# Hybrid encoder layer: u and Toeplitz loads by four groups, first state copies directly behind the scan, last key's scaling put behind the first weight splits

## Chip, core and metric

The kernel runs on one NeuronCore of a Trainium2 chip, as one program with one launch. The core has a matmul engine (TensorE, PE), a vector engine (VectorE, DVE), a scalar engine (ScalarE, ACT), a general engine (GpSimd, POOL) and a sync engine (SyncE, SP). They run side by side, each through its own list of instructions in order, and wait for each other on semaphores. Transfers are issued by SP, ACT and POOL and carried by 16 DMA engines that all three share. The metric is device time in microseconds of one execution. All data are 32-bit floats; products are made exact enough by splitting each operand into a high and a low part and adding three matmuls.

## What is computed

An encoder layer on two sequences of 512 tokens of width 1024: an S5 state-space branch beside windowed attention, then an MLP. What the change touches is the state-space branch and the norm of the keys:

```python
proj = h @ w_in
q, k, v, u, g_att, g_ssm = jnp.split(proj, IN_SPLITS, axis=-1)
k = rms_norm(k.reshape(bsz, seq_len, N_KV_HEADS, HEAD_DIM), k_gain)
...
bu_re = jnp.einsum('lgc,gpc->lgp', us, bb_re[d])
bu_im = jnp.einsum('lgc,gpc->lgp', us, bb_im[d])
_, _, h_re, h_im = lax.associative_scan(_complex_combine, (ar, ai, bu_re, bu_im),
                                        reverse=reverse, axis=0)
return (jnp.einsum('lgp,gcp->lgc', h_re, cr[d])
        - jnp.einsum('lgp,gcp->lgc', h_im, ci[d]))
...
y = jax.nn.gelu(lax.map(one_seq, u))
```

There are 64 groups of 16 channels with 64 states each, in two directions.

## The kernel before

The state-space branch is computed in chunks of 8 tokens. Within a chunk the outputs come from a Toeplitz matrix of each group (`toep`, written to DRAM earlier as `toep_scr`) times the inputs `u_sb`; what comes from earlier chunks is a table `ctab` times the chunk states `h`. The states come from a scan over 64 chunks on VectorE (L619 to L624, four instructions a step, 62 steps). Then the readout loop (L644 on) takes two groups at a time, 32 readouts `q`: `state_rows(q)` copies the states of two groups out of `h` into a tile `st` (L632 and L636 on VectorE, L634 on ScalarE for even `q`; for odd `q` VectorE copies both halves); TensorE multiplies `toep` with `u_sb` (L655) and `ctab` with `st` (L658) into a PSUM tile `sps`, of which there are two; ScalarE applies the Gelu (L665) into `ys`, and stores it (L640) after every second readout. State tiles are made two readouts ahead.

The loads of the loop are issued by POOL. `load_batch` (L598) loads `u_sb` and `toep` of eight groups, 512 KB each, into two buffers each; `load_table` (L607) loads `ctab` of four groups, 512 KB, into three buffers. Two batches and three tables are loaded ahead of the scan; then each load is issued when a batch (four readouts) or a table (two readouts) has been used. Each of them waits for TensorE to have read the buffer that it fills.

Between those matmuls TensorE works off a generator of filler products, `fillers()` (L248): columns of the input projection (L185; three products of column parts, with 24 matmuls each for one sequence), then the keys (L225). `pull(n)` takes n units of it, two for a column matmul and one for a key matmul. In a column, `split` (L167) casts a raw weight block to its high part on ScalarE (`c_hi`, L175) and subtracts it on VectorE (`c_lo`, L176). A product ends with a copy on ScalarE out of one of three PSUM tiles `acc` (L200 or L202). Behind the scan 64 units are pulled, then `state_rows(0)` and `state_rows(1)` are issued, then the loop begins. Two weight splits lie in those 64 units.

The keys come in eight tiles of 128 tokens. For each, ScalarE squares (L234), VectorE sums (L236), POOL adds and takes the power -1/2 (L238, L239), and VectorE scales (L242). The scaling of one tile is issued in the middle of the next tile's matmuls; that of the last one directly at its end. Then the first query and value weights are loaded and split (`whole_block`, L985; `w_hi` on ScalarE, `w_lo` L993 on VectorE), and the keys are copied by DMA to `kn` (L999).

In the readout loop the order of each engine but SP and POOL is the order of the code; at the keys' end and the first weights a scheduler sets the order, and on SP and POOL it does so throughout the loop.

Of the kernel before, what the change touches and what calls it, by code (L numbers as in the profile page):

```python
# [12 lines left out]
F32 = mybir.dt.float32  # L13
# [6 lines left out]
P = 128  # L20
# [5 lines left out]
NSEQ = 2  # L26
# [12 lines left out]
GROUPS = 64  # L39
STATE = 64  # L40
CH = 16
T = 8
NCHUNK = SEQ // T
SB = 8
SI = 4
SG = 4
SH = 2
# [16 lines left out]
def hybrid_layer(ctx, tc, x, rel, onehot, w_qkv, w_ug, vectors, lam, coefs, w_glu, w_out, ln2,  # L64
# [82 lines left out]
    dmask = vec_pad[:, 72:72 + CH]  # L147
    lbt = cf.tile([P, 2, SB, 64], F32, name="lbt")
    columns = [("u", U_BLK + c) for c in range(KT)] + [("a", GA_BLK + c) for c in range(KT)] + [("s", GS_BLK + c) for c in range(KT)]
    loaded, key_tiles, sigmoids = [], [], set()  # L150
    phase = {"next": 0, "raw": [], "units": 2 * 3 * KT * NSEQ * len(columns) + 3 * KT * NT, "gelu": False}

    def fetch():
# [60 lines left out]
    def key_products():  # L214
        later = None
        for t in range(NT):
            if t % 4 == 0:
                key_tiles.append(evp.tile([P, 4, N_KV, HD], F32, tag="ev", name="keys"))
            kt = key_tiles[-1][:, t % 4]
            ps = acc()[:, 0:CB]  # L220
            for n in range(3 * KT):
                k, p = divmod(n, 3)
                hi, lo = loaded[len(columns) + k // 4]
                act, wt = [(0, hi), (0, lo), (1, hi)][p]
                PE.matmul(ps, hT[t // 4][act][:, k, (t % 4) * P:(t % 4 + 1) * P], wt[:, k % 4, :],  # L225
                          start=n == 0, stop=n == 3 * KT - 1)
                if t == 0 and n in (2, 6):
                    split(n // 6)
                if n == 12 and later:
                    later()  # L230
                if n < 3 * KT - 1:
                    yield 1
            psv = ps.rearrange("p (h d) -> p h d", h=N_KV)
            S.activation(kt, psv, AF.Square, scale=HD ** -0.5)  # L234
            ms = small.tile([P, N_KV], F32, tag="ms", name="ms")
            V.reduce_sum(ms, kt, axis=AX.X)  # L236
            rk = small.tile([P, N_KV], F32, tag="rq", name="rk")
            GP.tensor_scalar_add(ms, ms, EPS)  # L238
            GP.tensor_tensor(rk, ms, neg_half[:, 0:N_KV], op=ALU.pow)  # L239

            def later(kt=kt, psv=psv, rk=rk):
                V.tensor_mul(kt, psv, rk[:, :, None].to_broadcast([P, N_KV, HD]))  # L242

            if t == NT - 1:
                later()
            yield 1

    def fillers():  # L248
# [18 lines left out]
    def pull(units):  # L267
        while units > 0:
            cost = next(filler, None)
            if cost is None:  # L270
                return
            units -= cost
            phase["units"] -= cost
# [175 lines left out]
    with tc.tile_pool(name="hst", bufs=1) as hp:  # L449
# [147 lines left out]
        with tc.tile_pool(name="ssmo", bufs=2) as sp:  # L597
            def load_batch(g0):  # L598

                u_sb = sp.tile([P, SB, NSEQ * NCHUNK], F32, tag="u_sb", name="u_sb")  # L600
                GP.dma_start(u_sb, u_scr[g0:g0 + SB].rearrange("g c t k -> (c t) g k"))
                toep = sp.tile([P, SB, T, CH], F32, tag="toep", name="toep")
                GP.dma_start(toep.rearrange("p g t c -> p g (t c)"),
                             toep_scr[:, :, g0:g0 + SB].rearrange("c t g n -> (c t) g n"))
                return u_sb, toep

            def load_table(g0):  # L607
                ctab = sp.tile([P, SI, 2, T * CH], F32, tag="ctab", name="ctab_in", bufs=3)
                GP.dma_start(ctab.rearrange("p g r n -> p (g r n)"),
                             ct_scr[:, g0:g0 + SI].rearrange("p g r n -> p (g r n)"))  # L610
                return ctab

            ahead = [load_batch(0)]
            ahead_c = [load_table(0), load_table(SI), load_table(2 * SI)]
            ahead.append(load_batch(SB))
            GP.dma_start(line_scr, line_one[:, None, :].to_broadcast([N_HEADS, P, LINE]))
            order.close()
            order.enter_context(tc.manual_schedule(engines={mybir.EngineType.PE, mybir.EngineType.Activation, mybir.EngineType.DVE}))
            for i in range(1, NCHUNK - 1):  # L619
                t1, t2 = [sp.tile([P, 2, GROUPS, NSEQ], F32, tag="st", name=n, bufs=3) for n in ("t1", "t2")]  # L620
                V.tensor_mul(t1, h[:, i], a8r)  # L621
                V.tensor_mul(t2, h[:, i, ::-1], a8i)
                V.tensor_add(t1, t1, h[:, i + 1])
                V.tensor_add(h[:, i + 1], t1, t2)  # L624
                pull(15)
            phase["gelu"] = True
            pull(64)
            def state_rows(q):
                st = sp.tile([P, 2, SH, NSEQ, NCHUNK], F32, tag="st", name="st", bufs=3)
                hv = h[:, :, :, q * SH:(q + 1) * SH, :].rearrange("p k r g s -> p r (g s) k")  # L630
                sv = st.rearrange("p r g s k -> p r (g s) k")
                V.tensor_copy(sv[64:128], hv[64:128, :, :, ::-1])  # L632
                if q % 2 == 0:
                    S.copy(sv[0:64], hv[0:64])  # L634
                else:
                    V.tensor_copy(sv[0:64], hv[0:64])  # L636
                return st

            def store_y(y, ga):
                S.dma_start(y_scr[:, :, ga:ga + SI].rearrange("t c g k -> (t c) (g k)"), y.rearrange("p g k -> p (g k)"))  # L640

            states = [state_rows(0), state_rows(1)]
            full = None
            for q in range(GROUPS // SH):  # L644
                g0 = q * SH
                if g0 % SB == 0:
                    u_sb, toep = ahead.pop(0)
                if g0 % SI == 0:
                    ctab = ahead_c.pop(0)
                    ys = sp.tile([P, SI, NSEQ * NCHUNK], F32, tag="ys", name="ys", bufs=3)  # L650
                st = states.pop(0)
                ps = sps()
                for g in range(SH):
                    o = ps[:, g * P:(g + 1) * P]
                    PE.matmul(o, toep[:, g0 % SB + g].rearrange("p t c -> p (t c)"), u_sb[:, g0 % SB + g, :],  # L655
                              start=True, stop=False)
                    for ri in range(2):
                        PE.matmul(o, ctab[:, g0 % SI + g, ri, 0:T * CH],  # L658
                                  st[:, ri, g].rearrange("p s k -> p (s k)"), start=False, stop=ri == 1)
                if q + 2 < GROUPS // SH:  # L660
                    states.append(state_rows(q + 2))
                if full:
                    store_y(*full)
                    full = None
                S.activation(ys[:, g0 % SI:g0 % SI + SH].rearrange("p g k -> p (g k)"), ps[:, 0:SH * P], AF.Gelu_apprx_tanh)  # L665
                if (g0 + SH) % SI == 0:
                    full = ys, g0 + SH - SI

                pull(-(-(phase["units"] - 84) // (GROUPS // SH - q)))
                if (g0 + SH) % SI == 0 and g0 + SH + 2 * SI < GROUPS:  # L670
                    ahead_c.append(load_table(g0 + SH + 2 * SI))
                if (g0 + SH) % SB == 0 and g0 + SH + SB < GROUPS:
                    ahead.append(load_batch(g0 + SH + SB))
            store_y(*full)
            pull(phase["units"])
            order.close()
# [67 lines left out]
    with tc.tile_pool(name="att", bufs=2, reuse_waits="tile") as ap, tc.tile_pool(name="attc", bufs=1, reuse_waits="tile") as ac:  # L744
# [240 lines left out]
        def whole_block(src, pool, tag, bufs):  # L985
            halves = []
            for e in range(2):
                hi, lo = [pool.tile([P, KT // 2, CB], F32R, tag=t, name=n) for t, n in (("c_hi", "w_hi"), ("c_lo", "w_lo"))]
                raw = ap.tile([P, KT // 2, CB], F32, tag=tag, name="w_in", bufs=bufs)
                SP.dma_start(raw, src[:, e * 4:e * 4 + 4, :])  # L990
                for sl in (slice(0, 2), slice(2, 4)):
                    S.copy(hi[:, sl, :], raw[:, sl, :])
                    V.tensor_sub(lo[:, sl, :], raw[:, sl, :], hi[:, sl, :].bitcast(F32))  # L993
                halves.append((hi, lo))
            return halves


        for sq in range(NSEQ):
            SP.dma_start(kn[:, sq * 4:sq * 4 + 4], key_tiles[sq])  # L999
        kd = key_copies(0, 0)  # L1000
        w_q = whole_block(w_qkv[Q_BLK], wq, "ya", 2)
        weights[0] = w_q
        w_v = whole_block(w_qkv[V_BLK], cpool, "p", 3)
        load_biases(0)
        rows = None
        for t in range(4):
# [653 lines left out]
```

## Time and profile before

| what | value |
|---|---|
| median of three runs | 1470.34 us (1469.9 to 1470.96) |
| the profiled execution | 1471.94 us |
| its span | 1470.2 us, 22081 instructions |
| scan on VectorE (first and last start of L621) | 214.1 to 324.4 us |
| readouts on TensorE (first and last start of L655) | 325.9 to 405.3 us |
| u_sb, toep and ctab_in loads by POOL | 8, 8 and 16, 512 KB each |
| median time of these to landing | 7.3, 8.1 and 6.9 us |

The span runs from the first to the last instruction; the execution's own time has a little around it. Times in the rows that the prediction shows are microseconds from the span's start. A row of the order of time is: start, busy time, engine, line, operation, output <- inputs, shapes, and in brackets the idle time before it with what ended it. A row of waits is: who waited <- for whom: total us, times, longest. A row of windows is: window, its length, busy us (and instructions) of PE, PEld, DVE, ACT and POOL, then the clock that TensorE was granted, the mean busy share of the DMA engines, and GB/s. A row of DMA issues is: output <- input, queue, kind, count, size of one, us from issue to landing.

### The profile page before, as it was taken

Reading aid. Unit: us, or ns where it says so; the run is one execution under the profiler, and the core shown is the slowest. Engines: PE = TensorE matmul, PEld = TensorE weight load, DVE = VectorE, ACT = ScalarE, POOL = GpSimd, SP = SyncE. Lnnn points to the kernel's source line nnn. Section 1 sums busy time; section 2 is a strip of 40 time slices with the busy share of each in tenths; the row PEclk is TensorE's granted clock in tenths of the full one; section 3 lists DMA queues with packets and bytes.
Section 4 is the critical chain, followed back from the end, with each engine's and each line's share of the span. In section 5 each row is a group of like instructions: output and inputs, shape, how many; then the busy total and the mean of one; then the engine's idle time right before and its main releaser. Section 6 shows DMA issues by size and latency. Waiting matters only on the chain.

```text
span 1470.2 us, 22081 instructions
## 1 busy us (share of the span) xinstructions
PE 1442.4 (98%) x8074; PEld 1231.2 (84%) x8074; DVE 1092.7 (74%) x1974; ACT 755.0 (51%) x1346; POOL 226.9 (15%) x372
## 2 busy tenths in 40 slices
PE   6999999999999999999999999999999999999998
PEld 4888888879999999987888878888888888888887
DVE  7989949995545899988984588777776588575653
ACT  6678851234335888786343355445444444333332
POOL 3044451003332433252100000000000000000000
PEclk9999999999999999999999999999999999999999
DMA  4455559428730533345552245444443894454441
GB/s 177 137 165 165 161 154 340 155 101 276 247 135 17 174 100 103 99 161 165 186 201 107 88 152 175 153 146 145 148 156 108 320 331 128 156 175 155 129 130 58
DMA packets 98269, 234.48 MB, mean 159 GB/s; under 512 B 11722, under 2 KB 23242, under 8 KB 98160
## 3 DMA queue, kind: packets, MB, share of 16 engines
q1 hardware_dynamic: 59088, 135.35, 28.3%
q0 software_dynamic: 15744, 47.23, 9.9%
q10 hardware_dynamic: 23328, 50.47, 9.3%
q8 instruction: 64, 1.05, 0.3%
q14 instruction: 45, 0.37, 0.1%
HBM read 163.78 MB, written 80.77 MB: 166 GB/s over the span
## 4 chain that ended last, share of the span: by engine, by line
PE 72%; DVE 14%; DMA 4%; issue 4%; ACT 3%; POOL 2%; SPq 0%; DVEq 0%; ACTq 0%; POOLq 0%
PE bank L117 13%; PE bank L118 13%; PE bank L116 13%; PE acc L185 6%; PE acc L821 5%; PE acc L117 3%; PE acc L118 3%; PE acc L116 3%; PE acc L123 2%; PE sps L553 2%; PE po L904 2%; DMA c_raw<-in_w_ug_dram 2%; PE sps L872 2%; PE tps L888 2%; DVE t L621 1%
## 5 line engine op out<-in xcount | busy, mean ns | idle before, releaser
L185 PE MATMUL acc<-act,c_hi 128*128 128x512 f32 x768 | 244.6, 396 | 1.0 <-DVE act L311 1.0
L117 PE MATMUL bank<-b_lo,a_hi 128*128 128x512 f32 x448 | 174.5, 389 | 0.1
L118 PE MATMUL bank<-b_hi,a_lo 128*128 128x512 f32 x448 | 174.3, 389 | 0.0
L116 PE MATMUL bank<-b_hi,a_hi 128*128 128x512 f32 x448 | 174.3, 389 | 0.0
L185 PEld LDWEIGHTS acc<-act,c_hi 128*128 128x128 f32 x768 | 143.0, 189 | 30.6 <-DVE act L311 2.4
L185 PE MATMUL acc<-act,c_lo 128*128 128x512 f32 x384 | 151.2, 394 | 0.0
L1520 ACT CAST a_hi<-d_a 128x1024 fp32r<-128x1024 f32 x56 | 59.0, 1054 | 178.7 <-PE bank L117 176.2
L116 PE MATMUL bank<-act,act 128*128 128x512 f32 x368 | 143.3, 389 | 0.5 <-ACT f_sum L1339 0.5
L117 PE MATMUL bank<-act,act 128*128 128x512 f32 x368 | 143.3, 389 | 0.2 <-DVE act L1298 0.2
L118 PE MATMUL bank<-act,act 128*128 128x512 f32 x368 | 143.2, 389 | 0.0
L1521 DVE TENSOR_TENSOR a_lo<-d_a,a_hi 128x1024 fp32r<-128x1024 f32 x56 | 68.5, 1223 | 96.3 <-ACT a_hi L1520 96.3
L821 PE MATMUL acc<-w_hi,act 128*128 128x256 f32 x512 | 114.1, 291 | 0.0
L117 PEld LDWEIGHTS bank<-b_lo,a_hi 128*128 128x128 f32 x448 | 84.1, 188 | 18.2 <-DVE b_lo L1521 0.7
L116 PEld LDWEIGHTS bank<-b_hi,a_hi 128*128 128x128 f32 x448 | 84.1, 188 | 17.6
L118 PEld LDWEIGHTS bank<-b_hi,a_lo 128*128 128x128 f32 x448 | 84.1, 188 | 17.3
L821 PEld LDWEIGHTS acc<-w_hi,act 128*128 128x128 f32 x512 | 87.1, 190 | 3.7
L185 PEld LDWEIGHTS acc<-act,c_lo 128*128 128x128 f32 x384 | 72.4, 189 | 14.6 <-DVE c_lo L176 0.5
L882 ACT ACTIVATE p<-p,nmx 128x257 f32<-128x257 f32 (+1 forms) x128 | 72.1, 564 | 19.7 <-DVE nmx L876 17.6
L116 PEld LDWEIGHTS bank<-act,act 128*128 128x128 f32 x368 | 69.1, 188 | 15.4 <-ACT f_sum L1339 0.9
L117 PEld LDWEIGHTS bank<-act,act 128*128 128x128 f32 x368 | 69.1, 188 | 14.7 <-DVE act L1298 0.5
L118 PEld LDWEIGHTS bank<-act,act 128*128 128x128 f32 x368 | 69.1, 188 | 14.3
L123 PE MATMUL acc<-act,gc_hi 128*128 128x512 f32 x256 | 81.1, 394 | 0.0
(333 smaller groups left out, 3427.2 us busy)
## 6 DMA issues: line engine op xcount, KB each, us to landing
d_a<-a_scr SPq DMA_DIRECT2D x56, 512.0 KB, 3.8
raws<-in_w_up_dram SPq DMA_DIRECT2D x32, 512.0 KB, 4.1
a_scr<-t ACTq DMA_DIRECT2D x64, 256.0 KB, 2.9
k<-in_w_down_dram SPq DMA_DIRECT2D x32, 512.0 KB, 5.9
c_raw<-in_w_ug_dram SPq DMA_DIRECT2D x48, 256.0 KB, 3.9
ct_scr<-ctab POOLq DMA_DIRECT2D x16, 512.0 KB, 4.7
ctab_in<-ct_scr POOLq DMA_DIRECT2D x16, 512.0 KB, 6.9
a_scr<-a ACTq DMA_DIRECT2D x32, 256.0 KB, 2.0
```

What stands on the lines that cost most here:

```text
L116: PE.matmul(ps, a[0], b[0], start=first, stop=False)
L117: PE.matmul(ps, a[0], b[1], start=False, stop=False)
L118: PE.matmul(ps, a[1], b[0], start=False, stop=last)
L123: PE.matmul(ps, w[wi][:, k, :], rows[yi], start=k + p == 0, stop=k == KT - 1 and p == 2)
L185: PE.matmul(ps, w[wi][:, k, :], hT[s][hi][:, k, :], start=n == 0, stop=n == 3 * KT - 1)
L553: PE.matmul(ps[:, i * P:(i + 1) * P], bm[:, ri, g, :], u_sb[:, gp * SH + g, :], start=True, stop=True)
L821: PE.matmul(self.ps, hT[sq][act][:, k, col:col + P], w[:, k % 4, :], start=i == 0, stop=i == 3 * KT - 1)
L872: PE.matmul(ps[:, 0:self.nk], qs, kk[:, self.k0 * P:self.k1 * P], start=i == 0, stop=i == 1)
L882: S.activation(p, p, AF.Exp, bias=self.nmx[:, h:h + 1], scale=-1.0, accum_out=self.sums[:, h, self.qb:self.qb + 1])
L888: PE.transpose(pt[:, h * P:(h + 1) * P], self.p[:, h, 1 + i * P:1 + (i + 1) * P], ident)
L1520: S.copy(hi, src)
L1521: V.tensor_sub(lo, src, hi.bitcast(F32))
```

## The change

```diff
@@ key_products @@
             if t == NT - 1:
-                later()
+                last_keys.append(later)
@@ load_batch @@
-                u_sb = sp.tile([P, SB, NSEQ * NCHUNK], F32, tag="u_sb", name="u_sb")
-                GP.dma_start(u_sb, u_scr[g0:g0 + SB].rearrange("g c t k -> (c t) g k"))
-                toep = sp.tile([P, SB, T, CH], F32, tag="toep", name="toep")
+                u_sb = sp.tile([P, SI, NSEQ * NCHUNK], F32, tag="u_sb", name="u_sb", bufs=4)
+                GP.dma_start(u_sb, u_scr[g0:g0 + SI].rearrange("g c t k -> (c t) g k"))
+                toep = sp.tile([P, SI, T, CH], F32, tag="toep", name="toep", bufs=4)
                 GP.dma_start(toep.rearrange("p g t c -> p g (t c)"),
-                             toep_scr[:, :, g0:g0 + SB].rearrange("c t g n -> (c t) g n"))
+                             toep_scr[:, :, g0:g0 + SI].rearrange("c t g n -> (c t) g n"))
@@ ahead of the scan @@
-            ahead = [load_batch(0)]
-            ahead_c = [load_table(0), load_table(SI), load_table(2 * SI)]
-            ahead.append(load_batch(SB))
+            ahead, ahead_c = [], []
+            for g0 in range(0, 3 * SI, SI):
+                ahead.append(load_batch(g0))
+                ahead_c.append(load_table(g0))
+            ahead.append(load_batch(3 * SI))
@@ behind the scan @@
             phase["gelu"] = True
-            pull(64)
...
             states = [state_rows(0), state_rows(1)]
+            pull(72)
@@ readout loop @@
-                if g0 % SB == 0:
+                if g0 % SI == 0:
                     u_sb, toep = ahead.pop(0)
-                if g0 % SI == 0:
                     ctab = ahead_c.pop(0)
...
-                if (g0 + SH) % SB == 0 and g0 + SH + SB < GROUPS:
-                    ahead.append(load_batch(g0 + SH + SB))
+                if (g0 + SH) % SI == 0 and g0 + SH + 3 * SI < GROUPS:
+                    ahead.append(load_batch(g0 + SH + 3 * SI))
@@ first weights @@
-        for sq in range(NSEQ):
-            SP.dma_start(kn[:, sq * 4:sq * 4 + 4], key_tiles[sq])
+        SP.dma_start(kn[:, 0:4], key_tiles[0])
         kd = key_copies(0, 0)
         w_q = whole_block(w_qkv[Q_BLK], wq, "ya", 2)
         weights[0] = w_q
         w_v = whole_block(w_qkv[V_BLK], cpool, "p", 3)
+        last_keys.pop()()
+        SP.dma_start(kn[:, 4:8], key_tiles[1])
```

SB is 8 and SI is 4 groups. u_sb and toep are now loaded by four groups, 256 KB each, into four buffers, so that the memory is the same; there are 16 loads of each instead of 8. Behind the scan the state copies of the first two readouts are issued first, then 72 units of filler instead of 64. The last key's scaling and the copy of the second four key tiles are written behind the splits of the first weights.

On ScalarE at the scan's end stood (L634 is the state copy, `sg` a gate column, `ys` the Gelu's output):

```order
L200 COPY sg<-acc 128x512
L209 DMA gs_scr<-sg 128x1024
L175 CAST c_hi<-c_raw 128x512 x2
L634 COPY st<-h 64x512 x2
L665 ACT_TABLE_LOAD
L665 ACTIVATE ys<-sps 128x256 x2
L200 COPY sg<-acc 128x512
```

and stands now (the state copy is L636, the Gelu L667):

```order
L636 COPY st<-h 64x512
L200 COPY sg<-acc 128x512
L209 DMA gs_scr<-sg 128x1024
L175 CAST c_hi<-c_raw 128x512 x2
L636 COPY st<-h 64x512
L667 ACT_TABLE_LOAD
L667 ACTIVATE ys<-sps 128x256
L200 COPY sg<-acc 128x512
L667 ACTIVATE ys<-sps 128x256
```

The first state copy moved ahead of a gate copy, its store and two casts, and a second gate copy came between the first two Gelus. On VectorE, likewise, the three copies of the first two state tiles (L634 and L638 of the changed kernel) moved ahead of the two splits that stood behind the last scan step.

On POOL, the loads in the middle of the loop stood so:

```order
L601 DMA u_sb<-u_scr 128x8x128
L609 DMA ctab_in<-ct_scr 128x1024
L603 DMA toep<-toep_scr 128x1024
L609 DMA ctab_in<-ct_scr 128x1024
L601 DMA u_sb<-u_scr 128x8x128
```

and stand now:

```order
L601 DMA u_sb<-u_scr 128x4x128
L609 DMA ctab_in<-ct_scr 128x1024
L603 DMA toep<-toep_scr 128x512
L601 DMA u_sb<-u_scr 128x4x128
L609 DMA ctab_in<-ct_scr 128x1024
```

Each table load is now between two half loads; the table's own size, buffers and place of issue are as before.

On VectorE, at the end of the keys and the first weights, stood (L242 is the scaling of a key tile, L993 the weight split):

```order
L993 TENSOR_TENSOR w_lo<-w_in,w_hi 128x512 x3
L236 TENSOR_REDUCE ms<-keys 128x4
L993 TENSOR_TENSOR w_lo<-w_in,w_hi 128x512
L242 TENSOR_TENSOR keys<-acc,rk 128x256
L993 TENSOR_TENSOR w_lo<-w_in,w_hi 128x512 x2
L831 TENSOR_REDUCE ms<-sq 128x4
```

and stands now:

```order
L995 TENSOR_TENSOR w_lo<-w_in,w_hi 128x512 x3
L236 TENSOR_REDUCE ms<-keys 128x4
L995 TENSOR_TENSOR w_lo<-w_in,w_hi 128x512
L242 TENSOR_TENSOR keys<-acc,rk 128x256
L995 TENSOR_TENSOR w_lo<-w_in,w_hi 128x512 x2
L833 TENSOR_REDUCE ms<-sq 128x4
```

Nothing moved here but the line numbers: the scheduler puts the last scaling at the same place.

More of the change, by code (lines that the diff above doesn't have):

```diff
@@ L149, in hybrid_layer @@
     columns = [("u", U_BLK + c) for c in range(KT)] + [("a", GA_BLK + c) for c in range(KT)] + [("s", GS_BLK + c) for c in range(KT)]
-    loaded, key_tiles, sigmoids = [], [], set()
+    loaded, key_tiles, last_keys, sigmoids = [], [], [], set()
     phase = {"next": 0, "raw": [], "units": 2 * 3 * KT * NSEQ * len(columns) + 3 * KT * NT, "gelu": False}
@@ L654, in hybrid_layer @@
                     o = ps[:, g * P:(g + 1) * P]
-                    PE.matmul(o, toep[:, g0 % SB + g].rearrange("p t c -> p (t c)"), u_sb[:, g0 % SB + g, :],
+                    PE.matmul(o, toep[:, g0 % SI + g].rearrange("p t c -> p (t c)"), u_sb[:, g0 % SI + g, :],
                               start=True, stop=False)
```

## The prediction

> **What bounds the kernel now.** I read the page first, for the engine that is never idle, then the waits on TensorE between 325 and 430 us, where all three edits lie, and then the order of time around each wait.
>
> ```profile
> PE 1442.4 (98%) x8074; PEld 1231.2 (84%) x8074; DVE 1092.7 (74%) x1974; ACT 755.0 (51%) x1346; POOL 226.9 (15%) x372
> PE sps L655 <- DMA toep<-toep_scr: 3.0, 1, 3.0
> PE sps L658 <- ACT st L634: 1.7, 1, 1.7
> PE acc L117 <- DVE w_lo L993: 1.0, 1, 1.0
> ```
>
> TensorE is busy 98% of the span, so a change that removes no matmul can win only what TensorE idles near it: 3.0 + 1.7 + 1.0 = 5.7 us, three waits, one for each edit. Whatever is saved here moves everything behind it forward, since TensorE is the bound from there to the end.
>
> The first wait, at the scan's end, in the order of time on TensorE, ScalarE and VectorE:
>
> ```profile
> 325.93 0.38 PE L655 MATMUL sps<-u_sb,toep 128*128 128x128 f32 x2
> 328.01 0.68 PE L658 MATMUL sps<-st,ctab_in 128*128 128x128 f32 x4 [1.70 <-ACT st L634]
> 330.35 0.38 PE L655 MATMUL sps<-u_sb,toep 128*128 128x128 f32 x2
> 322.04 0.59 ACT L200 COPY sg<-acc 128x512 f32<-128x512 f32 x1 [4.84 <-PE acc L185]
> 322.66 0.33 ACTq L209 DMA_DIRECT2D gs_scr<-sg  x1
> 323.67 1.35 ACT L175 CAST c_hi<-c_raw 128x512 fp32r<-128x512 f32 x2 [1.04 <-DMA c_raw<-in_w_ug_dram]
> 326.02 2.04 ACT L634 COPY st<-h 64x512 f32<-64x512 f32 x2 [1.00 <-DVE h L624]
> 328.08 1.28 ACT L665 ACT_TABLE_LOAD   x1
> 329.40 0.39 ACT L665 ACTIVATE ys<-sps 128x256 f32<-128x256 f32 x1
> 325.51 0.42 DVE L624 TENSOR_TENSOR h<-t,t 128x256 f32<-128x256 f32 x1
> 325.86 1.28 DVE L176 TENSOR_TENSOR c_lo<-c_raw,c_hi 128x512 fp32r<-128x512 f32 x2
> 327.17 1.40 DVE L632 COPY st<-h 64x512 f32<-64x512 f32 x2
> ```
>
> The last scan step ends at 325.93, exactly when TensorE has used up its filler products and reaches the first readout. The readout needs state tile 0, half from ScalarE and half from VectorE. The waits view names ScalarE, but ScalarE's first copy was over at about 326.02 + 2.04/2 = 327.04. VectorE did two splits (1.28 us) before its half, and that half ended near 327.17 + 0.75 = 327.9: the wait belongs to the two splits.
>
> The second wait, with the filler step before it, the pitch of an ordinary readout (340.06 to 342.33), and the loads that it waited for:
>
> ```profile
> 340.06 0.39 PE L655 MATMUL sps<-u_sb,toep 128*128 128x128 f32 x2
> 342.33 0.38 PE L655 MATMUL sps<-u_sb,toep 128*128 128x128 f32 x2
> 383.54 0.28 PE L225 MATMUL acc<-c_lo,act 128*128 128x256 f32 x1
> 386.85 0.46 PE L655 MATMUL sps<-u_sb,toep 128*128 128x128 f32 x2 [3.02 <-DMA toep<-toep_scr]
> 390.42 0.63 PE L655 MATMUL sps<-u_sb,toep 128*128 128x128 f32 x2
> 373.55 0.91 POOL L601 DMA_DIRECT2D u_sb<-u_scr  x1 [3.44 <-PE sps L655]
> 374.45 0.72 POOL L609 DMA_DIRECT2D ctab_in<-ct_scr  x1
> 375.16 0.77 POOL L603 DMA_DIRECT2D toep<-toep_scr  x1
> u_sb<-u_scr POOLq DMA_DIRECT2D x1, 512.0 KB, 8.2
> ctab_in<-ct_scr POOLq DMA_DIRECT2D x1, 512.0 KB, 10.6
> toep<-toep_scr POOLq DMA_DIRECT2D x1, 512.0 KB, 11.6
> 326.00:340.00 14.00, 12.30 (x85) 11.19 (x84) 9.19 (x13) 7.69 (x11) 2.73 (x4) 1.00 0.44 127
> 340.00:372.00 32.00, 31.93 (x226) 29.05 (x226) 16.88 (x23) 14.52 (x26) 9.71 (x13) 1.00 0.96 326
> 388.00:390.00 2.00, 2.00 (x12) 2.00 (x11) 0.00 (x0) 0.58 (x2) 0.00 (x0) 0.50 0.98 383
> 390.00:392.00 2.00, 2.00 (x14) 2.00 (x14) 1.74 (x3) 0.19 (x1) 1.19 (x2) 0.70 0.20 80
> ```
>
> The 512 KB Toeplitz load issued at 375.16 lands 11.6 us later, at 386.8, and TensorE starts there; without it the readout was due at about 383.8. The last three numbers of a window are granted clock, DMA share and GB/s: the DMA engines are 96% busy from 340 to 372 but 44% from 326 to 340. And the wait costs more than its 3.02 us: behind it the granted clock is 0.50 for 2 us and 0.70 for 2 us, so (0.50 + 0.30) x 2 = 1.6 us more.
>
> **Part 1, states ahead of the splits.** VectorE's half of state 0 now starts at 325.93 and is there at 326.7; ScalarE's half, put ahead of the gate copy, still waits for the scan and is there at 327.04. TensorE has four more filler products: (330.35 - 328.01) holds five products and a readout, 340.06 to 342.33 four and a readout, so one is 0.2 us and the readout comes at about 325.93 + 0.9 = 326.8. Its first matmul needs no state; the wait left is 0 to 0.1 us. Saved: 1.7 us, without the 0.9 us of products, which only change places.
>
> But ScalarE now does, behind that copy and ahead of its first Gelu, what it did from 322.04 to 325.02 before: 327.04 + gate copy 0.59 + DMA issue 0.33 + casts 1.35 + state copy 1.02 + table load 1.28 + Gelu 0.39 = 332.0. Readouts use two PSUM buffers, so the third readout waits for that first Gelu, and it is due at 326.8 + 2 x 2.27 = 331.3. Before, the Gelu ended at 329.8. So a new wait of 0.7 us at the third readout; 0 if the issue and the engine's starts overlap, 1.2 if each handover costs 0.1 us more. The second gate copy, also ahead of the second Gelu now, ends before the fourth readout is due at 334.3. The delayed gate copy frees its bank 5 us later; there are three, and each product takes 24 matmuls, so nobody waits. Its 512 KB store follows it by those 5 us into a window in which the DMA engines have room, and SyncE's next column loads wait for the moved splits, some 3 us later, a column ahead of their use. **Net: 1.0 us gained (0.4 to 1.7).**
>
> **Part 2, loads by four groups.** Bytes and buffer space are the same; a buffer of four groups comes free after two readouts, and its data are used six readouts later (13.6 us by the pitch) rather than four (9.1 us). The landings of 8.2 and 11.6 us then fit with room for u and Toeplitz: 3.02 + 1.6 = 4.6 us are freed. POOL issues twelve more loads in the loop; a half u load costs it between 0.5 and 0.91 us, in idle time. The first loads are issued one readout pair earlier in the loop, in the window that was 44% busy.
>
> What is late next is **ctab**: three buffers as before, a lead of four readouts as before, and its row says 374.45 + 10.6 = 385.05 while its readout was due at 383.9. It was itself 1.2 us late, covered by the Toeplitz load. In the change 256 KB less stand ahead of it on POOL's queue, counted from the end of the eighth batch of four groups (u 3 x 256, Toeplitz 2 x 256, ctab 3 x 512 against u 2 x 512, Toeplitz 512, ctab 3 x 512, with itself). The end of the ctab at 385.05 and of the Toeplitz behind it at 386.76 give 1.7 us for 512 KB, so it lands 0.85 us earlier; the half u issue adds 0 to 0.4. Left: 0 to 1.2 us, and I take 0.4, with full clock. **Net: 4.2 us gained (3.4 to 4.9).**
>
> Here a rule of the Trainium skill speaks against the change. DMA: Bandwidth & Descriptors, section "Bandwidth", wants transfers of at least 1 MiB for 75% of the peak and takes small ones as dominated by a fixed cost. By it, halving 512 KB loads on saturated DMA engines loses bandwidth and the term turns negative, the last rival below; the 1.7 us from one landing to the next show no room for a large fixed share.
>
> **Part 3, the last keys.** The program's order shows no move: on VectorE the last key's scaling stands where it stood, ahead of the last two weight splits, and the queue of SyncE has the same rows.
>
> ```profile
> 421.48 0.42 DVE L242 TENSOR_TENSOR keys<-acc,rk 128x256 f32<-128x256 f32 x1 [1.23 <-POOL rk L239]
> 421.82 1.28 DVE L993 TENSOR_TENSOR w_lo<-w_in,w_hi 128x512 fp32r<-128x512 f32 x2
> ```
>
> VectorE sits 1.23 us waiting for POOL's power at the scaling, and the split behind it is what TensorE waits 1.0 us for. That all hangs on TensorE's own progress, so it shifts along. **Net: 0.**
>
> **Sum.** 1.0 + 4.2 + 0 = 5.2 us. Of the profiled execution, 1471.94 us with a span of 1470.2, that leaves 1466.7. Its median of three runs is 1470.34, 1.6 us under the profiled one; I apply the same 5.2 us there: **1465.1 us**. About 0.2% (2.9 us) is the least that a measurement of this kernel can tell from no change.
>
> **The rivals.**
> - *Forecast, 0.55:* 4 to 6.5 us gained, 1463.8 to 1466.3.
> - *The ctab wait takes the Toeplitz wait's place, 0.2.* For it: the DMA share of 0.96, and the 1.2 us that ctab is late in the trace. A stall of 2 to 3 us on ctab leaves 1.0 + 4.6 - 2 to 3 = 2.6 to 3.6 us, and 1.0 if the clock is halved again: 1466.7 to 1469.3. The trace has full clock after 1.70 us of idling and half after 3.02; between them no row decides. TensorE: Matmul & The Clock Gate, section "Part 1: The HAM clock gate (the "warmup" mystery)", puts it at one idle window of about 3.4 us that runs freely. By that rule a stall of 2 us mostly keeps its clock, and this rival ends at its better edge.
> - *The scan ends later, 0.1.* By the order with its waits, the 4 MB line_scr transfer now waits for an earlier load before it is issued, so it falls later on the loads that the scan's splits need.
>
> ```profile
> line_scr<-line_one POOLq DMA_DIRECT2D x1, 4096.0 KB, 26.5
> DVE c_lo L176 <- ACT c_hi L175: 2.3, 2, 1.6
> ```
>
> VectorE lost 2.3 us there before; as much again would hold state 0, and with TensorE arriving within 0.1 us of it, would cost that in full: 1467.4.
> - *All of it, 0.1:* no Gelu wait, no ctab wait, part 3 working through some wait after all: 1.7 + 4.6 to 5.6 = 6.3 to 7.3 us, 1463.0 to 1464.0.
> - *Slower, 0.05: a fixed cost of each load on POOL's queue.* The twelve added loads each hold the queue for a time f. The row below bounds f: 14 KB stores issued every 0.5 us still land in 1.7 us, so nothing piles up at 0.5 us each.
>
> ```profile
> lag_scr<-ks POOLq DMA_DIRECT2D x64, 14.0 KB, 1.7
> ```
>
> With f = 0.5, the most that this allows, the queue is 6 us later at the end of the loop. Ctab's 1.2 - 0.85 us grow to 6.4, in stalls long enough to halve the clock twice (3.2 us): 9.6 lost against 4.6 + 1.0 won, 1474.3. It turns the sign from f = 0.2 to 0.3 on.
>
> **The numbers.** Faster by over 0.2%: forecast 0.55, all of it 0.1, most of the late scan 0.05, the better edge of the ctab rival 0.08, together 0.78. Slower 0.05. The rest, 0.17, is within 0.2%. The range 1463.0 to 1468.4 takes in the forecast, all of it, the late scan and more than half of the ctab rival.
>
> **What would show it.** Right: no Toeplitz row among TensorE's waits, granted clock 1.00 from 386 to 392, a wait on ys of 0.3 to 1.2 us at the third readout, the wait on st under 0.2 us, the w_lo wait still 1.0. Wrong: a ctab wait over 1.5 us near the 23rd to 27th readout; the last scan step more than 0.3 us later; landings of half loads not well under those of whole ones.

## The result, and the profile after

The changed kernel takes 1466.23 us, the median of seven runs (1464.11 to 1466.88), beside 1470.34 us for seven runs of the kernel before (1467.13 to 1474.84): a ratio of 0.9967, with a 95% interval of 0.9953 to 0.9982. That is 4.9 us less by the ratio (2.6 to 6.9), 4.1 us by the medians, and 5.2 us was forecast. The profiled execution takes 1466.23 us against 1471.94, with a span of 1464.4 us.

The waits of TensorE between 320 and 430 us in the changed kernel (who waited, for whom, total us, times, longest), after them its busy time from the page:

```profile
PE acc L117 <- DVE w_lo L995: 1.0, 1, 1.0
PE sps L660 <- ACT st L636: 0.2, 1, 0.2
PE sps L657 <- ACT ys L667: 0.2, 1, 0.2
PE 1441.0 (98%) x8074; PEld 1229.6 (84%) x8074; DVE 1092.6 (75%) x1974; ACT 754.7 (52%) x1346; POOL 236.5 (16%) x388
```

The Toeplitz wait of 3.0 us is gone, the state wait is down from 1.7 to 0.2, the low weight half still costs 1.0, and one small wait is new, on the Gelu's tile `ys`. POOL has 16 more instructions, the added loads, and no row of TensorE's waits names them.

The scan's end, in the order of time on TensorE, ScalarE and VectorE of the changed kernel:

```profile
326.41 0.38 PE L657 MATMUL sps<-u_sb,toep 128*128 128x128 f32 x2
326.97 0.71 PE L660 MATMUL sps<-st,ctab_in 128*128 128x128 f32 x4 [0.18 <-ACT st L636]
331.71 0.49 PE L657 MATMUL sps<-u_sb,toep 128*128 128x128 f32 x2 [0.17 <-ACT ys L667]
325.84 1.08 ACT L636 COPY st<-h 64x512 f32<-64x512 f32 x1 [9.06 <-DVE h L626]
326.83 0.57 ACT L200 COPY sg<-acc 128x512 f32<-128x512 f32 x1
327.80 1.14 ACT L175 CAST c_hi<-c_raw 128x512 fp32r<-128x512 f32 x2 [0.40 <-ACT sg L200]
329.98 1.28 ACT L667 ACT_TABLE_LOAD   x1
331.28 0.38 ACT L667 ACTIVATE ys<-sps 128x256 f32<-128x256 f32 x1
325.34 0.42 DVE L626 TENSOR_TENSOR h<-t,t 128x256 f32<-128x256 f32 x1
325.86 1.43 DVE L634 COPY st<-h 64x512 f32<-64x512 f32 x2
```

The scan's last step starts at 325.34 us (325.51 before), so nothing holds the scan up. Both halves of state 0 start behind it at once, and the readout waits 0.18 us. The first Gelu is over at 331.66 us, 0.12 us after the third readout was ready for it.

The windows in which the Toeplitz load was late before (the last three numbers are granted clock, DMA share and GB/s), the loads of the loop, and the three loads of the place of the old wait:

```profile
340.00:372.00 32.00, 32.00 (x231) 29.64 (x230) 16.23 (x22) 15.77 (x28) 15.83 (x22) 1.00 0.96 322
386.00:388.00 2.00, 2.00 (x20) 2.00 (x20) 1.48 (x4) 1.07 (x3) 1.75 (x2) 1.00 0.95 358
388.00:390.00 2.00, 2.00 (x21) 2.00 (x19) 1.47 (x2) 0.33 (x1) 0.00 (x0) 1.00 0.78 244
390.00:392.00 2.00, 2.00 (x20) 2.00 (x19) 0.83 (x2) 1.67 (x3) 0.34 (x1) 1.00 0.50 196
...
ctab_in<-ct_scr POOLq DMA_DIRECT2D x13, 512.0 KB, 6.8
u_sb<-u_scr POOLq DMA_DIRECT2D x12, 256.0 KB, 6.6
toep<-toep_scr POOLq DMA_DIRECT2D x12, 256.0 KB, 7.1
...
372.45 0.88 POOL L609 DMA_DIRECT2D ctab_in<-ct_scr  x1
373.32 0.76 POOL L603 DMA_DIRECT2D toep<-toep_scr  x1
381.82 0.39 PE L657 MATMUL sps<-u_sb,toep 128*128 128x128 f32 x2
382.04 0.61 PE L660 MATMUL sps<-st,ctab_in 128*128 128x128 f32 x4
ctab_in<-ct_scr POOLq DMA_DIRECT2D x1, 512.0 KB, 9.3
toep<-toep_scr POOLq DMA_DIRECT2D x1, 256.0 KB, 9.7
```

TensorE is busy in every microsecond of these windows and has full clock. The DMA engines are as busy as before (0.96). In the median the half loads land little sooner than the whole ones (u 6.6 us against 6.9, Toeplitz 7.1 against 8.1). The table issued at 372.45 lands 9.3 us later, at 381.75, and is first read at 382.04: in time, by 0.3 us.

The first query product on TensorE shows what the stage won in these two profiles: it starts at 410.25 us (L823) against 416.92 (L821), 6.7 us earlier. The state wait (1.5 us less), the Toeplitz wait (3.0) and the half clock (1.6), less the new `ys` wait, make 6.0 of it. Of the other 0.7, 0.3 lies ahead of all three waits: up to 325.50 us TensorE has been busy for 312.36 us, against 312.03 before. The rest was not followed up. Of the 6.7 us, 0.9 is lost again behind, since the span is 5.8 us shorter; 0.7 of that is a wait in the down projection:

```profile
PE bank L117 <- DVE b_lo L1524: 0.7, 1, 0.7
```

### The profile page after: what moved, and what is told of

Same layout as the page of the kernel before. It is cut to its first block, busy times and chain, and to the rows that moved or that the text cites. A ratio compares the mean times of both kernels' runs of the same rounds, so it can differ in the third digit from the quotient of the medians.

```text
span 1464.4 us, 22111 instructions
## 1 busy us (share of the span) xinstructions
PE 1441.0 (98%) x8074; PEld 1229.6 (84%) x8074; DVE 1092.6 (75%) x1974; ACT 754.7 (52%) x1346; POOL 236.5 (16%) x388
## 4 chain that ended last, share of the span: by engine, by line
PE 76%; DVE 12%; DMA 4%; ACT 4%; issue 2%; POOL 1%; SPq 0%; DVEq 0%; ACTq 0%; POOLq 0%
PE bank L117 13%; PE bank L118 13%; PE bank L116 13%; PE acc L185 7%; PE acc L823 5%; PE acc L117 3%; PE acc L118 3%; PE acc L116 3%; DMA c_raw<-in_w_ug_dram 2%; PE acc L123 2%; PE sps L553 2%; PE sps L660 2%; PE po L906 2%; PE acc L225 2%; PE sps L874 2%
## 5 line engine op out<-in xcount | busy, mean ns | idle before, releaser
L823 PE MATMUL acc<-w_hi,act 128*128 128x256 f32 x512 | 114.2, 291 | 0.0
L823 PEld LDWEIGHTS acc<-w_hi,act 128*128 128x128 f32 x512 | 87.1, 190 | 3.7
```

The lines of the kernel that those rows point to most:

```text
L823: PE.matmul(self.ps, hT[sq][act][:, k, col:col + P], w[:, k % 4, :], start=i == 0, stop=i == 3 * KT - 1)
```

## The experiments

Twelve runs of eight kernels were made in three sessions: the first runs of the three parts alone and of the moved key in the first; the old lead in small pieces, the whole loads with lead, the fourth table buffer and the changed kernel in the second; parts 1 and 2 again, the moved key again and the changed kernel in the third. The kernel before was timed in each session (29, 20 and 26 times). A ratio is to the kernel before in the same session, with its 95% interval; a number of us less without another source is worked out from it. The list of timed executions gives the mean granted clock of each, to three digits, and that turned out to matter: of the 75 executions of the kernel before, 46 show 1.000 (median 1468.5 us) and 29 show less (median 1471.2 us); the median of all is 1469.2. One spell of the half clock costs 1.6 to 1.7 us, so an execution at 1.000 had none in full.

**Part 1 alone, twice.** On the kernel before:

```diff
             phase["gelu"] = True
-            pull(64)
...
             states = [state_rows(0), state_rows(1)]
+            pull(72)
```

> Part 1 alone, on the kernel before. Theory (the parts are separate, each gives back its own wait): the state wait at the first readout falls from 1.7 us to under 0.3; the wait on the first Gelu at the third readout is 0.2 us as in the changed kernel, not the 0.7 us that the prediction set; the Toeplitz wait of 3.0 us and the half clock behind it stay. Together 1.2 to 1.5 us less than before, so that TensorE's first query product starts that much earlier. Rival (the parts share a limit: what the states win only makes the readouts come earlier on the same loads): the Toeplitz wait grows by what the states won, to 4 us or more, and the time is that of before, within 0.3 us.

> Part 1 alone once more, in one call with part 2 alone and with both. The first time part 1 alone won 0.7 us, part 2 alone 2.5 us, and the changed kernel 4.8 and 5.3 us, more than their sum. Theory (the parts add, and the gap is the scatter of the half clock): part 1 alone wins 1.0 to 2.0 us. Rival (part 1 alone only brings TensorE to the late Toeplitz load earlier, and what it wins is lost there): 0.8 us or less, with more executions that show a granted clock under 1.000 than before has.

First 1468.23 us, ratio 0.9995 (0.9986 to 1.0005), 0.7 us less; then 1468.94 us, ratio 0.9994 (0.9984 to 1.0005), 0.9 us less. Waits and clock of the first profile, then of the second:

```profile
PE sps L656 <- DMA toep<-toep_scr: 1.9, 1, 1.9
PE acc L117 <- DVE w_lo L994: 1.2, 1, 1.2
384.00:386.00 2.00, 2.00 (x20) 2.00 (x19) 0.81 (x2) 0.77 (x2) 0.33 (x1) 1.00 0.97 315
```

```profile
362.90 0.46 PE L656 MATMUL sps<-u_sb,toep 128*128 128x128 f32 x2 [1.00 <-DMA toep<-toep_scr]
384.21 0.46 PE L656 MATMUL sps<-u_sb,toep 128*128 128x128 f32 x2 [2.80 <-DMA toep<-toep_scr]
386.00:388.00 2.00, 2.00 (x11) 2.00 (x11) 0.31 (x1) 0.77 (x2) 0.00 (x0) 0.50 0.93 367
```

The state wait is gone and the Gelu wait does not show at all, so part 1 does what it says. In time, no expectation was met as written: 0.7 us lies between the first theory's 1.2 to 1.5 and its rival's 0.3, 0.9 us between the second theory's 1.0 to 2.0 and its rival's 0.8, and neither is clear of no change. The Toeplitz wait stays, 1.9 us with full clock in one execution, 2.8 and 1.0 us with the half clock in the other. By the timed executions 12 of 24 have a clock under 1.000 (29 of 75 before, no clear difference). Within one class of clock part 1 wins 1.3 us (1467.2 against 1468.5 at 1.000) and 1.4 us (1469.8 against 1471.2 below it). The medians of all runs are only 0.7 us apart. The split is made by something that is seen only after the run, and if part 1 itself tips some executions into the half clock, it flatters part 1; the 12 of 24 do not exclude that. That the win is lost at the Toeplitz load is not shown: its waits are 1.9 and 3.8 us here, and 3.0 and 3.2 in the two profiles with the order of before.

**Part 2 alone, twice.** The changed kernel without the lines of part 1 and part 3, that is, the kernel before with the lines of `load_batch`, of the first loads and of the loop as in the diff above:

```diff
-                u_sb = sp.tile([P, SB, NSEQ * NCHUNK], F32, tag="u_sb", name="u_sb")
+                u_sb = sp.tile([P, SI, NSEQ * NCHUNK], F32, tag="u_sb", name="u_sb", bufs=4)
...
-                if (g0 + SH) % SB == 0 and g0 + SH + SB < GROUPS:
-                    ahead.append(load_batch(g0 + SH + SB))
+                if (g0 + SH) % SI == 0 and g0 + SH + 3 * SI < GROUPS:
+                    ahead.append(load_batch(g0 + SH + 3 * SI))
```

> Part 2 alone, on the kernel before. Theory: no Toeplitz wait and no table wait over 0.2 us, full clock from 384 to 394 us, the state wait of 1.7 us stays, because VectorE still makes two splits ahead of its half of the state. 4.6 to 5.2 us less than before in that stage. Rival (the table load takes over as the late one when the readouts are not also moved earlier or later by the states): a wait on the tables of 0.3 to 1.2 us near the 23rd to 27th readout and 3.4 to 4.2 us less.

> Part 2 alone once more. Theory (the parts add): it wins 3.0 to 4.0 us, so that it makes up the changed kernel's gain together with part 1 alone, within 0.8 us. Rival (part 2 wins more once part 1 is in): 2.7 us or less, and a gap to the changed kernel's gain of over 1 us that part 1 alone does not fill.

First 1466.3 us, ratio 0.9983 (0.9975 to 0.9991), 2.5 us less; then 1466.68 us, ratio 0.9981 (0.9973 to 0.999), 2.8 us less. The first profile:

```profile
PE sps L659 <- ACT st L636: 1.3, 1, 1.3
PE acc L117 <- DVE w_lo L994: 1.3, 1, 1.3
386.00:388.00 2.00, 2.00 (x20) 2.00 (x19) 1.51 (x3) 0.98 (x2) 1.32 (x2) 1.00 0.76 289
```

No wait on Toeplitz, inputs or tables is left, and the clock is full. So the mechanism is as the theory says, and neither theory has its size: both expected 3.4 us or more for the first run, and the theory of the second 3.0 to 4.0. What is won is nearer to the wait of a full-clock execution (1.9 us above) than to that of the profiled one. Only 4 of 23 executions show a clock under 1.000; among the others the median is 1466.15, 2.3 us under before's 1468.5.

**Part 3 alone.** On the kernel before, the lines of part 3 as in the diff above (`last_keys`, and the copy of the second four key tiles behind it) and nothing else:

```diff
-                later()
+                last_keys.append(later)
...
         w_v = whole_block(w_qkv[V_BLK], cpool, "p", 3)
+        last_keys.pop()()
```

> Part 3 alone, on the kernel before. Every engine has the same instructions in the same order as before. Theory: no change, under 0.5 us either way, and the wait on the low weight half stays at 1.0 us. Rival (something that the order does not show, such as the time at which the keys are read): the wait on the low half falls, and 0.5 to 1.0 us are won. The size of the difference is also what this comparison calls nothing.

1470.67 us, ratio 1.0007 (0.9998 to 1.0016). Its waits and the clock behind the Toeplitz load:

```profile
PE sps L655 <- DMA toep<-toep_scr: 3.2, 1, 3.2
PE sps L658 <- ACT st L634: 1.3, 1, 1.3
PE acc L117 <- DVE w_lo L993: 1.2, 1, 1.2
386.00:388.00 2.00, 2.00 (x12) 2.00 (x11) 0.00 (x0) 0.38 (x1) 0.00 (x0) 0.50 0.96 374
```

No wait goes away, so part 3 wins nothing. The 1.0 us by which its ratio is above 1 is inside the interval, for the same instructions in the same order (by the medians it is 1.8 us): that much is nothing here. It is also a second look at the order of before: the state wait is 1.3 us here and 1.7 there, the Toeplitz wait 3.2 and 3.0.

**The lead, or the size of a load?** One kernel keeps the pieces of 256 KB and takes away the added lead:

```diff
-                u_sb = sp.tile([P, SI, NSEQ * NCHUNK], F32, tag="u_sb", name="u_sb", bufs=4)
+                u_sb = sp.tile([P, SI, NSEQ * NCHUNK], F32, tag="u_sb", name="u_sb", bufs=3)
...
-                if (g0 + SH) % SI == 0 and g0 + SH + 3 * SI < GROUPS:
-                    ahead.append(load_batch(g0 + SH + 3 * SI))
+                if (g0 + SH) % SI == 0 and g0 + SH + 2 * SI < GROUPS:
+                    ahead.append(load_batch(g0 + SH + 2 * SI))
```

> The changed kernel with three buffers of four groups for u and Toeplitz in place of four, so that each is loaded two batches (four readouts, about 9.1 us) ahead, as in the kernel before, but in pieces of 256 KB. Theory (the six readouts of lead win): a wait on u or Toeplitz of 0.5 to 2 us comes back near the 21st to 27th readout, and the time is 1 to 3 us above the changed kernel. Rival (the smaller pieces win: with half of the bytes ahead on the queue, a load lands in under 9.1 us): no such wait over 0.3 us, and the time of the changed kernel within 1 us.

The other keeps the pieces of 512 KB and adds lead, eight readouts with three buffers, and so half as much memory again (with part 1):

```diff
-                toep = sp.tile([P, SB, T, CH], F32, tag="toep", name="toep")
+                toep = sp.tile([P, SB, T, CH], F32, tag="toep", name="toep", bufs=3)
...
             ahead.append(load_batch(SB))
+            ahead.append(load_batch(2 * SB))
...
-                if (g0 + SH) % SB == 0 and g0 + SH + SB < GROUPS:
-                    ahead.append(load_batch(g0 + SH + SB))
+                if (g0 + SH) % SB == 0 and g0 + SH + 2 * SB < GROUPS:
+                    ahead.append(load_batch(g0 + SH + 2 * SB))
```

> Part 1, with u and Toeplitz loaded by eight groups as before, but into three buffers each, two batches (eight readouts, about 18 us) ahead. Theory (lead is what was missing, the size of a load is nothing): no Toeplitz wait, full clock from 384 to 394 us, the time of the changed kernel within 1 us. Rival (whole loads hold the tables back that are queued behind them): no Toeplitz wait either, but a wait on the tables of 1 us or more in its place, and 1 to 3 us above the changed kernel.

And the changed kernel itself in the same session:

> The changed kernel once more, beside the kernels of this call. The kernel before had the half clock in 11 of its 29 last timed executions by the mean granted clock (0.999 or less; median 1470.3 us) and not in the other 18 (1.000; median 1468.2 us). Theory (the change wins the Toeplitz wait in every execution, and the half clock only in those that had it): 3.0 to 4.5 us under the median of before, a granted clock of 1.000 in nearly all executions. Rival (the wait itself comes and goes, and in a typical execution of before there is little to win): under 2.5 us.

Small pieces with the old lead: 1466.69 us, ratio 0.9981 (0.9971 to 0.9991). Whole loads with lead: 1465.69 us, ratio 0.9972 (0.996 to 0.9984). The changed kernel: 1464.48 us, ratio 0.9964 (0.995 to 0.9977), with 1.000 in four of five executions; it is 5.3 us less (3.4 to 7.3) and 4.7 by the medians, above the theory's 3.0 to 4.5 and far from the rival's 2.5. The waits of small pieces with the old lead, and the load that the first waited for:

```profile
371.64 0.77 POOL L603 DMA_DIRECT2D toep<-toep_scr  x1
toep<-toep_scr POOLq DMA_DIRECT2D x1, 256.0 KB, 9.6
381.33 0.46 PE L656 MATMUL sps<-u_sb,toep 128*128 128x128 f32 x2 [1.04 <-DMA toep<-toep_scr]
PE acc L822 <- DVE w_lo L994: 0.8, 1, 0.8
```

The waits of whole loads with lead, and the loads issued together there at 370 to 372 us:

```profile
381.07 0.68 PE L660 MATMUL sps<-st,ctab_in 128*128 128x128 f32 x4 [0.35 <-DMA ctab_in<-ct_scr]
u_sb<-u_scr POOLq DMA_DIRECT2D x1, 512.0 KB, 8.2
ctab_in<-ct_scr POOLq DMA_DIRECT2D x1, 512.0 KB, 9.8
toep<-toep_scr POOLq DMA_DIRECT2D x1, 512.0 KB, 11.2
```

In small pieces the Toeplitz load of this place lands after 9.6 us instead of 10.4 to 11.8 in the four profiles with the old loads, and that cuts the wait to 1.04 us, with full clock; it does not end it. The time is 2.2 us above the changed kernel, as that theory has it (1 to 3), but only about half of that is the Toeplitz wait: a second wait on a low weight half, 0.8 us, stands beside it. With whole loads and two batches of lead it takes 11.2 us, and nobody waits for it. So lead alone, here eight readouts, ends the Toeplitz wait, and smaller pieces alone do not. But the table behind a whole u load takes 9.8 us and is then 0.35 us late; behind a half load it takes 9.3, 8.3 and 9.1 us in three profiles of the changed kernel, and is in time in all three. Pieces buy that much: more than the first theory of that run allows, less than its rival's 1 us. Between the times of whole loads with lead and of the changed kernel, 1.2 us apart, the intervals do not decide.

**A fourth table buffer,** on the changed kernel:

```diff
-                ctab = sp.tile([P, SI, 2, T * CH], F32, tag="ctab", name="ctab_in", bufs=3)
+                ctab = sp.tile([P, SI, 2, T * CH], F32, tag="ctab", name="ctab_in", bufs=4)
...
-                if (g0 + SH) % SI == 0 and g0 + SH + 2 * SI < GROUPS:
-                    ahead_c.append(load_table(g0 + SH + 2 * SI))
+                if (g0 + SH) % SI == 0 and g0 + SH + 3 * SI < GROUPS:
+                    ahead_c.append(load_table(g0 + SH + 3 * SI))
```

> The changed kernel with a fourth table buffer, so that tables are loaded three batches ahead as u and Toeplitz are. In the profile of the changed kernel the table of the 25th readout lands 0.1 to 0.3 us ahead of its use. Theory (tables are at the edge, and late in some executions, which makes the spread of the changed kernel, 1464.1 to 1466.9 us): the table lands 3 us or more ahead of its use, and the median falls by 0.5 to 1.5 us. Rival (the spread comes from elsewhere): the table lands earlier as well, and the time stays within 0.5 us.

1464.95 us, ratio 0.9968 (0.9956 to 0.9979), against 1464.48 us for the changed kernel in the same session. Each table is now issued two readouts earlier: the one issued at 372.28 us lands 8.4 us later, at 380.7, and is first read at 386.45. Nothing is won, and the six runs still spread over 2.4 us: tables are near the edge, but not over it, and the spread of the changed kernel has another source.

**The last key really moved,** on the changed kernel, with an order forced between the last weight split and the scaling:

```diff
-                    V.tensor_sub(lo[:, sl, :], raw[:, sl, :], hi[:, sl, :].bitcast(F32))
+                    last_split[0] = V.tensor_sub(lo[:, sl, :], raw[:, sl, :], hi[:, sl, :].bitcast(F32))
...
-        last_keys.pop()()
+        with tc.issue_after(last_split[0].ins):
+            last_keys.pop()()
```

> The changed kernel, with the last keys' scaling really queued behind the last two weight splits on VectorE, by an added order between the two. Theory (the splits stand behind a scaling that waits 1.2 us for GpSimd's power): the wait on the low weight half, 1.0 us, falls to under 0.2, and 0.8 to 1.0 us are won on the changed kernel. Rival (the product that waits is held by ScalarE's copies to the high halves, or the bank that the late scaling keeps is needed next): the wait goes over to another releaser, at the value products or at the next bank, and the time stays within 0.3 us of the changed kernel.

> The changed kernel with the last keys' scaling behind the last two splits, beside the changed kernel in one call. Theory (its wait of 1.0 us on the low weight half is a wait of the whole kernel): 0.7 to 1.2 us under the changed kernel. Rival (what is won there is lost in the down projection, whose weights come by transfers: a wait of 0.2 to 1.3 us on their low halves comes and goes between the profiles): within 0.4 us of the changed kernel.

> The changed kernel, third time, as the measure for the other three of this call. Both theories: 4 to 5.5 us under before.

First 1464.02 us, ratio 0.9965 (0.9951 to 0.9978), with no changed kernel beside it in that session; then, beside the changed kernel, 1464.03 us, ratio 0.9967 (0.9955 to 0.9979), where the changed kernel had 1465.38 us, ratio 0.9975 (0.9966 to 0.9985). VectorE in the changed kernel, then in this one:

```profile
414.81 0.42 DVE L242 TENSOR_TENSOR keys<-acc,rk 128x256 f32<-128x256 f32 x1 [1.23 <-POOL rk L239]
415.15 1.28 DVE L995 TENSOR_TENSOR w_lo<-w_in,w_hi 128x512 fp32r<-128x512 f32 x2
```

```profile
412.91 1.89 DVE L997 TENSOR_TENSOR w_lo<-w_in,w_hi 128x512 fp32r<-128x512 f32 x3
415.11 0.42 DVE L242 TENSOR_TENSOR keys<-acc,rk 128x256 f32<-128x256 f32 x1 [0.32 <-POOL rk L239]
```

The splits now run in the time in which VectorE sat waiting for POOL's power, and the row of the `w_lo` wait is gone from both profiles. The spans of the two profiles are 1462.2 and 1461.9 us, those of three profiles of the changed kernel 1464.4, 1464.6 and 1462.8. The medians are 1.35 us apart in the one session that has both, a little over the theory's 0.7 to 1.2; over all sessions of this section 14 runs of the changed kernel have a median of 1465.0 and 12 of this one 1464.0. Drawing both sets anew many times puts that difference at 0.4 to 2.1 us (95%). As part 3 alone moved by 1.0 us without a moved instruction, the gone wait of 1.0 us is the firmer evidence, and the time agrees with it. It is the fastest version measured here, and the one that does what part 3 says.

The third session also has both parts alone and together. Part 1 wins 0.9 us, part 2 2.8, and the changed kernel 3.7 (2.2 to 5.0), under the 4 to 5.5 that was expected of it. 0.9 and 2.8 are 3.7: the parts add, as the theories of the second runs of part 1 and part 2 have it, though neither part has the size that they gave it. Each of the three has an interval of more than 1 us to either side, so this excludes only a large gap. The gap seen across sessions, 0.7 and 2.5 in the first against 4.9 and 5.3 for the changed kernel elsewhere, did not come again.

## Why the prediction was right, and where it was not

**Part 1.** The state wait went nearly as forecast (0.18 us at the readout). The Gelu wait came at the place that was named, at 0.17 us instead of 0.7. The mis-sized step is the sum on ScalarE that put the Gelu's end at 332.0 us and the third readout at 331.3. In the profile the Gelu ends at 331.66, because the first state copy was over at 326.92, not 327.04, and the two casts took 1.14 us, not 1.35; and the third readout was ready only at 331.54. The 0.17 us is also below the 0.3 us that was named as the least sign of being right. The first readout came at 326.41, not at 326.8, since TensorE was already ahead; so 0.18 us of the state wait was left, against 0 to 0.1. Forecast net 1.0 us, in a range of 0.4 to 1.7; measured 1.3 us at equal clock and 0.7 over all runs.

**Part 2.** The mechanism is as told: Toeplitz was late for want of lead, six readouts are enough, and the table was what came next. Three sizes were off. The range's upper end of 4.9 us is more than the 4.6 that its own terms give. The table was put 0.4 us late, and is 0.3, 1.3 and 0.5 us early in three profiles; it was predicted from one landing of 10.6 us, less 0.85, and this load lands after 8.3 to 9.3 us in the change. And the landings of half loads were to be well under those of whole ones; in the median they hardly are (6.6 against 6.9 for u, 7.1 against 8.1 for Toeplitz). That was listed as a sign of being wrong, and it was a poor sign: the kernel with the old lead shows that landing sooner did only part of the work.

**The step that failed most is the price of the half clock.** The prediction took 1.6 us for it out of the profiled execution (1.7 with the window from 386 to 388 us), and then applied the whole 5.2 us to the median of the runs, although it had noted that the profiled execution was 1.6 us above that median. The half clock is not in every execution: 29 of 75 of the kernel before show a mean clock under 1.000, and of the four profiles with the old loads, three have it (waits of 2.80, 3.02 and 3.23 us) and one has not (1.92 us). The wait of 3.02 us itself is that of an execution with the half clock. So part 2 alone won 2.5 and 2.8 us, where 4.2 (3.4 to 4.9) was forecast.

The mark counts too many. In the profile with a fourth table buffer the mean is 0.999 too, and there the clock is full up to the last matmul, which ends at 1460.5 us; it is 0.64 from 1462 to 1464 us, where that costs nothing. And of 75 executions of the kernels whose profiles show no wait on a load over 1.04 us (part 2 alone, the changed kernel and all that were made from it, and whole loads with more lead), 13 show less than 1.000. So the share of executions that lose clock in the readouts is between some 16 (29 less 13) and 29 of 75. With 16/75 to 29/75 of 1.6 us, 0.3 to 0.6, in place of the whole, the prediction's sum would have been 3.9 to 4.2.

At a clock of 1.000 the parts add up: part 1 wins 1.3 us, part 2 2.3, and the change 3.5 (1468.5 to 1465.0). The rest of the gain is put down to executions that no longer lose clock; that is argued, not shown. The 14 runs of the changed kernel in the last two sessions have a median of 1465.0, 4.2 us under the 1469.2 of the 75 runs; drawing both sets anew many times puts that at 3.1 to 4.7 us (95%), so 5.2 is too much. That it still came close to the 4.9 and 4.1 us of the result is in part luck: the Gelu wait was put 0.5 us and the table 0.4 us too dear, against some 1.0 to 1.3 us too much for the half clock and a Toeplitz wait of 3.0 us where the full-clock profile has 1.9; and an interval of 2.6 to 6.9 us tells none of these apart.

**Part 3.** As forecast, nothing: no order changed, and no wait. The reason given, that VectorE sits behind POOL's power at the scaling, was right as well, since moving the scaling for real ends the wait.

**The rivals.** A table wait in place of the Toeplitz wait: no profile of the changed kernel has one, though whole loads with lead had 0.35 us of it. A later scan: its last step is 0.17 us earlier. A fixed cost of each load that turns the sign: POOL's twelve added loads are there, and no wait came of them. The rule that was weighed against the change, the Trainium skill's DMA: Bandwidth & Descriptors, section "Bandwidth", on transfers of at least 1 MiB, did not bear here (its fixed cost is said of transfers under 64 KB, and these are of 256 KB): with half the size the window from 340 to 372 us moves 322 GB/s at a DMA share of 0.96, against 326 and 0.96.

**Still open:** the wait on `b_lo` in the down projection, 0.7 us in the profile after, 0.2 to 1.3 in those of the experiments, and not among the waits of the kernel before. The run of part 3 alone, with the order of before, has 0.2 us of it, so it needs no change of order. No experiment was aimed at it, and whether the change feeds it is not known.

## What to carry to other kernels

The transfer that landed late on busy queues here was cured by issuing it earlier; if the memory is to stay the same, buffers of half the size, twice as many, give the earlier issue, and that was worth more than the shorter transfers. A stall of 2 to 3 us on TensorE had two prices here, with and without a halved clock, and the profiled execution shows one of them: before a sum made in one profile is applied to a median, see in how many executions its parts occur. And an edit of the code's order under a scheduler is an edit only if the order of instructions on the engine changed; where it did not, force it and measure that instead.

## What the hardware showed unexpectedly

In the readouts the clock was halved behind idle times of TensorE of 2.80, 3.02 and 3.23 us, each time for about 3.5 us (387.7 to 391.2 in the kernel before), and not behind 1.92, 1.70 or 1.04. The Trainium skill, TensorE: Matmul & The Clock Gate, section "Part 1: The HAM clock gate (the "warmup" mystery)", gives at least one idle window of about 3.4 us; here less was enough. Whether the same wait halves the clock or not differed between executions of one kernel, as the wait itself did: in one and the same order of instructions it was 1.9 us in one profile and 2.8 and 1.0 us in another. The end of the kernel shows the same with nothing else going on: behind the last matmul the clock drops after 5.2, 5.2 and 2.3 us in three profiles of the changed kernel, and after 2.0 to 5.3 us in all 14 profiles. So in these traces no one length of idling decides it; what does was not found.
